# A decoder block on one core: the first pair's channel tiles share each piece of x, the rows come behind x, and turned values, tables and weight sums change places in the written order

## The chip, the cores and the metric

The kernel runs on one core of one Trainium2 chip. The metric is the device time of one execution in microseconds (us), the median over runs; lower is better.

## What is computed

One decoder block on a sequence of 1024 tokens with 1024 channels, in float32:

```python
h = rms_norm(x, mix_norm_g)
proj = h @ w_in                                   # 1024 -> 5888
z_a, q, k, v, gate_logits = split(proj)
y_a = chunked_spatial_gating(gelu(z_a), gmlp_norm_g, w_spatial, b_spatial)
q, k = apply_partial_rope(q, cos, sin), apply_partial_rope(k, cos, sin)
y_b = dilated_mixture_attention(q, k, v)          # 3 groups of 4 heads
merged = sigmoid(g_A) * (y_a @ w_branch_a) + sigmoid(g_B) * (y_b @ w_branch_b)
x = x + merged @ w_out
h2 = rms_norm(x, ffn_norm_g)
a, val = split(h2 @ w_up)                         # 1024 -> 2 x 2816
x = x + (gelu(causal_dwconv3(a)) * val) @ w_down
return rms_norm(x, final_norm_g)
```

In the spatial gating, `z_a` splits into `u` and `v`; `v` is RMS-normed over its 768 channels, mixed along 128 positions by a lower triangular matrix, and multiplied into `u`. The rotation (rope) turns the first 16 of 64 dimensions of q and k by tables of sines and cosines of the positions.

## The kernel before

**Operands in two parts.** TensorE multiplies in a float format shorter than float32, so each operand is split into a high part (ACT copies it into the short format) and a remainder (DVE, sometimes GpSimd, subtracts). Three matmuls per product, `PASSES`, take high x high, high x remainder and remainder x high. A weight tile or a tile of x must therefore pass through DMA, ACT and DVE before all three can run.

**Pairs and Strassen products.** The input projection is cut into 23 pairs of 128 columns. For most pairs a Winograd-Strassen scheme forms seven products P1 to P7 of quarter matrices, each of 12 matmuls of 128x512 (`in_product`, L512). Their left operands (A11, A12, A22, S1 to S4) are the normed x or sums of its quarters, their right ones are quarters of the pair's weights or sums of those (`weight_sums`, L270: three subtractions on DVE for P6, one for P4). `in_ahead` (L326) loads weights ahead and makes the operands of the next products; `in_split` (L300) gives the two halves of one such operand as two calls.

**The first two pairs are plain.** The left operands need the norm of x, which is not known at the start. So pairs 0 and 1 multiply raw x (times the gain), without Strassen, and the row scale is applied later, when the values are turned. Each pair has two channel tiles i = 0, 1 and two token halves h = 0, 1; `plain_step` (L575) issues the three matmuls of one piece of x, a [128 channels x 512 tokens] tile `x_half(kt, h)` of 256 KB. `raw_left` (L456) splits a piece. Beside this the rows of x (the other layout) are loaded into `rows_of`, ACT squares and sums them (`square_row`, L377), GpSimd takes the root (`root`, L384), DVE puts the scales on a diagonal (`diagonal`, L392), eight matmuls spread them over the partitions (`spread`, L401), and DVE scales x in place (`scale_x`, L468).

**An order written out by hand.** TensorE's order is that of the program everywhere. DVE's and ACT's are too from the start to product i = 10 (`ORDERED`), and again from the end of the mixing to `end_order(last_b)` (L2063); in between, and after, a scheduler chooses. `beginning` (L1069) writes the first part, then the loop from L1235 calls for each product i `in_ahead`, `in_product` and `meanwhile(i)` (L1186). Pair 2 (`FIRST`) has i = 0 to 6 (P1, P2, P6, P7, P5, P4, P3), pair 3 has i = 7 to 13 (P1, P6, P2, P7, P5, P4, P3). An engine works its list in order: an instruction that waits holds all behind it.

**Ticks.** `tick` (L213) is called twice in each product, after 6 and after 12 matmuls, and runs what `after(lag, fn)` has put there. So the turned values are placed: `turn_v` (L631) has TensorE transpose four 128x128 blocks into one of two PSUM banks (`tr_tile`), and ACT empties it into V (two instructions of L641 for pairs 0 and 1, one of L646 for pair 2). `norm_v` (L650), `spatial` (L655) and the rotation (`rope`, L729, with four stores on SP) are placed the same way.

**Tables.** `rot_tables` (L2236) makes a chain of 39 small steps on DVE (L2253), the last of which are two sines on ACT; 16 wide copies on ACT (L2299, `wide`); and four turns (`turns`: four transposes, L2316, and a copy by ACT, L2317). `some(n)` takes the next n steps of the chain.

**The up-projection.** It uses the same seven products per tile of 128 columns (`up_product`, L1838; `up_ahead` for loads and operands). `beginning_up` writes products 0 to 22 by hand. In a hand-written stretch remainders on DVE go to a list, `waiting`, and `low(n)` issues n of them; `end_order` issues the rest and ends the stretch. Products i = 23 to 29 are P6 of tile 4, P1 of 5, P7 and P5 of 4, P2 of 5, P4 and P3 of 4.

Of the kernel before, what the change touches and what calls it, by code (L numbers as in the profile page):

```python
# [20 lines left out]
P = 128  # L21
# [72 lines left out]
def block_kernel(  # L94
# [259 lines left out]
    raws[0, 0] = wt.tile([P, KT, P], F32, name="wr_0_0", tag="wr")  # L354
    for k in range(2):
        ks = slice(k * QK, (k + 1) * QK)
        nc.sync.dma_start(raws[0, 0][:, ks], w_in[0][:, ks])
        load_x(0, range(k * QK, (k + 1) * QK))
    in_load(0, 1)
    load_x(1, range(QK))  # L360
    load_rows(0)
    load_x(1, range(QK, KT))
# [212 lines left out]
    def plain_step(n, h, i, k, kt):  # L575
# [7 lines left out]
        for p, (w, a) in enumerate(PASSES):  # L583
            nc.tensor.matmul(
                acc, plain_ops[n, k, i][:, w, kt, :], raw_x[h, k * QK + kt][:, a, :],
                start=k == 0 and kt == 0 and p == 0,
                stop=k == 1 and kt == QK - 1 and p == 2,
                skip_group_check=True,
            )
# [131 lines left out]
    def turned(n):  # L721
# [24 lines left out]
        after(4, rope)  # L746
# [322 lines left out]
    def beginning():  # L1069
# [5 lines left out]
        chain = iter(chain)  # L1075

        def some(n):
            for _, fn in zip(range(n), chain):
                fn()
# [78 lines left out]
        product(1, 0, 1)  # L1158
# [23 lines left out]
        return some, wide, turns, a22  # L1182

    late = {}

    def meanwhile(i):  # L1186
# [6 lines left out]
        elif i == 2:  # L1193
            for _, lo in late["S1"]:
                lo()
            late["P4"] = in_split(FIRST, "P4")
            in_ready["op"] += 1
            late["P4"][0]()
        elif i == 3:
            late["P4"][1]()  # L1200
# [3 lines left out]
            for hi, _ in late["S4"]:  # L1204
                hi()
        elif i == 4:
            in_ahead(i, 9, 3)
            for _, lo in late["S4"]:
                lo()
            x_stack.close()  # L1210
# [4 lines left out]
            for b in range(0, NB, 2):  # L1215
                after(3 + b // 2, lambda b=b: turn_v(1, C[1], b))
                after(7 + b // 2, lambda b=b: turn_v(0, C[0], b))
        elif i in (5, 6):
            in_ahead(i, 9, 4)
        elif i == 7:  # L1220
            some(15)
        elif i == 9:
            some(99)
            for fn in wide:
                fn()
        elif i in (11, 12):
            turns.pop(0)()
# [6 lines left out]
    some, wide, turns, a22 = beginning()  # L1234
    for i, (n, name) in enumerate(in_order):  # L1235
        in_ahead(i, 9, 4 if i > ORDERED - 4 else 0)
# [1135 lines left out]
```

## Time and profile before

| what | value |
|---|---|
| median of 3 runs | 1392.97 us (1392.63 to 1394.66) |
| the profiled execution | 1394.24 us, span from its first to its last instruction 1392.5 us |
| mean granted TensorE clock | 0.995 |
| busy: TensorE, DVE, ACT, GpSimd | 1367.2, 1032.1, 653.9, 297.6 us |
| DMA | 237.01 MB, mean 170 GB/s |

PE is TensorE's matmuls, PEld its weight loads, DVE the vector engine, ACT the scalar engine, POOL GpSimd, SP the engine that issues most DMAs. A row of the order of time has the start in us, the length in us, engine, line, operation, output and inputs, shape, count of merged instructions, and in brackets the idle time of the engine before it with what ended it. In the chain of waits, "start, length, what". A matmul's length overlaps the next one's, so rates are read from start to start.

### The profile page before, as it was taken

How to read it: one execution, taken by the hardware profiler on the slowest of the kernel's cores; microseconds unless marked ns; L12 is line 12 of the kernel's file. 1: busy time of each engine (PE TensorE's matmuls, PEld its weight loads, DVE VectorE, ACT ScalarE, POOL GpSimd, SP SyncE). 2: the span in 40 equal slices, each digit the busy share in tenths (PEclk: the TensorE clock that was granted, in tenths of full speed). 3: DMA queues.
4: the chain of work that ended last, by engine and by line, in shares of the span. 5: the costliest groups of instructions: out<-in, count | busy, mean ns of one | idle time of the engine just before them, and what ended most of it. 6: DMA issues, size and time to landing. Idle time of an engine off the chain costs nothing.

```text
span 1392.5 us, 19210 instructions
## 1 busy us (share of the span) xinstructions
PE 1367.2 (98%) x6434; PEld 1131.8 (81%) x6434; DVE 1032.1 (74%) x1880; ACT 653.9 (47%) x1289; POOL 297.6 (21%) x295
## 2 busy tenths in 40 slices
PE   8979999999999999999999999999999999999997
PEld 7867788888888888888788887888888888888886
DVE  7967677686887987867889887766766667675674
ACT  7663255555554332634646443433333335455453
POOL 0111000000231000120001136555566553000002
PEclk9999999999999999999999999999999999999999
DMA  9423535354435987694843132333333327986563
GB/s 362 78 65 107 181 112 166 113 163 141 135 121 193 330 295 257 218 299 141 285 132 105 38 113 107 106 106 105 103 107 118 121 84 244 392 312 228 194 208 121
DMA packets 143875, 237.01 MB, mean 170 GB/s; under 512 B 13728, under 2 KB 57504, under 8 KB 143776
## 3 DMA queue, kind: packets, MB, share of 16 engines
q1 hardware_dynamic: 141248, 231.53, 49.5%
q0 software_dynamic: 1088, 2.10, 0.9%
q10 hardware_dynamic: 1440, 2.16, 0.4%
q8 instruction: 51, 0.84, 0.3%
q14 instruction: 48, 0.39, 0.1%
HBM read 167.77 MB, written 64.29 MB: 167 GB/s over the span
## 4 chain that ended last, share of the span: by engine, by line
PE 83%; DVE 6%; issue 3%; ACT 3%; DMA 2%; POOL 1%; SPq 0%; POOLq 0%; DVEq 0%; ACTq 0%
PE in_P L523 26%; PE uP L1849 18%; PE dn L2106 13%; PE up L1849 7%; PE pa L1322 5%; PE wo_P L1683 4%; PE pu L864 2%; PE pu L1829 2%; PE pb L1322 2%; DMA X<-in_xt_dram 1%; PE pp L848 1%; PE sc L809 1%; PE sc L810 1%; PE pm L673 1%; POOL fm_f L2227 1%
## 5 line engine op out<-in xcount | busy, mean ns | idle before, releaser
L523 PE MATMUL in_P<-R,G 128*128 128x512 f32 x1008 | 245.6, 396 | 0.0
L523 PEld LDWEIGHTS in_P<-R,G 128*128 128x128 f32 x1008 | 186.2, 189 | 36.3
L2106 PE MATMUL dn<-R 128*128 128x512 f32 x924 | 209.6, 389 | 0.0
L2106 PEld LDWEIGHTS dn<-R 128*128 128x128 f32 x924 | 173.5, 188 | 36.0
L168 ACT ACTIVATE R<-up 128x512 fp32r<-128x512 f32 x130 | 78.4, 627 | 118.6 <-DVE up L277 40.9
L307 ACT ACTIVATE G<-wr 128x512 fp32r<-128x512 f32 x126 | 79.0, 628 | 106.6 <-PE in_P L523 68.4
L523 PE MATMUL in_P<-G,G 128*128 128x512 f32 x504 | 123.8, 397 | 1.2 <-DVE C L550 1.2
L1849 PE MATMUL uP<-G,R 128*128 128x512 f32 x504 | 121.5, 390 | 1.8 <-DVE Y L1870 1.6
L1849 PE MATMUL up<-G,R 128*128 128x512 f32 x504 | 121.5, 391 | 0.1
L1849 PE MATMUL uP<-R 128*128 128x512 f32 x504 | 121.1, 389 | 0.0
L308 DVE TENSOR_TENSOR G<-wr,G 128x512 fp32r<-128x512 f32 x126 | 88.2, 700 | 33.5 <-ACT G L307 32.6
L1849 PEld LDWEIGHTS uP<-G,R 128*128 128x128 f32 x504 | 94.4, 188 | 22.5 <-DVE Y L1870 2.1
L1849 PEld LDWEIGHTS up<-G,R 128*128 128x128 f32 x504 | 94.6, 188 | 21.0 <-POOL R L169 0.6
L523 PEld LDWEIGHTS in_P<-G,G 128*128 128x128 f32 x504 | 94.1, 190 | 20.9 <-issue 1.8
L1849 PEld LDWEIGHTS uP<-R 128*128 128x128 f32 x504 | 94.6, 188 | 19.6
L169 POOL TENSOR_TENSOR R<-up,R 128x512 fp32r<-128x512 f32 x55 | 84.0, 1527 | 74.6 <-ACT R L168 74.6
L169 DVE TENSOR_TENSOR R<-up,R 128x512 fp32r<-128x512 f32 x75 | 62.3, 833 | 19.1 <-ACT R L168 18.9
L168 ACT ACTIVATE R<-db 128x512 fp32r<-128x512 f32 x77 | 48.1, 626 | 56.8 <-PE dn L2106 46.0
L169 DVE TENSOR_TENSOR R<-db,R 128x512 fp32r<-128x512 f32 x77 | 53.9, 703 | 26.0 <-ACT R L168 25.9
L1322 PE MATMUL pa<-R,G 128*128 128x512 f32 x288 | 67.9, 389 | 0.0
L523 PE MATMUL in_P<-G 128*128 128x512 f32 x252 | 62.4, 394 | 1.2 <-ACT G L307 1.2
L1322 PEld LDWEIGHTS pa<-R,G 128*128 128x128 f32 x288 | 54.1, 188 | 11.2
(279 smaller groups left out, 2398.2 us busy)
## 6 DMA issues: line engine op xcount, KB each, us to landing
wr<-in_w_in_dram SPq DMA_DIRECT2D x45, 512.0 KB, 4.3
up<-in_w_up_dram SPq DMA_DIRECT2D x44, 512.0 KB, 3.6
dA<-gd SPq DMA_DIRECT2D x55, 256.0 KB, 5.0
wd<-in_w_down_dram SPq DMA_DIRECT2D x44, 256.0 KB, 5.2
wT<-wd SPq DMA_DIRECT2D x44, 256.0 KB, 3.8
dS<-gS SPq DMA_DIRECT2D x44, 256.0 KB, 4.2
db<-wT SPq DMA_DIRECT2D x44, 256.0 KB, 4.5
gd<-Y SPq DMA_DIRECT2D x42, 256.0 KB, 2.0
```

The lines of the kernel that those rows point to most:

```text
L168: nc.scalar.activation(hi, src, AF.Copy)
L169: fn = lambda: lo_eng.tensor_tensor(lo, src, f32(hi), ALU.subtract)
L307: lambda: nc.scalar.activation(op[:, 0], src, AF.Copy),
L308: lambda: nc.vector.tensor_tensor(op[:, 1], src, f32(op[:, 0]), ALU.subtract),
L523: nc.tensor.matmul(acc, op[:, w, kt, :], left[LEFT[name], kt][:, a, :], start=opened and i == 0, stop=i == len(HIGH_FIRST) - 1, skip_group ...
L673: nc.tensor.matmul(pm[:, o : o + P], v[:, c * P : (c + 1) * P], wspT[:, c * 2 // 3, :], start=True, stop=True,)
L864: nc.tensor.matmul(pu[:, h * HD : (h + 1) * HD], self.pT[:, i, :], vt[:, h * HD : (h + 1) * HD], start=i % n == 0, stop=i % n == n - 1,)
L1322: nc.tensor.matmul(acc, unit[a][kt // 4][:, kt % 4, :], two(R, 8 * h + kt)[:, b, :], start=n == 0 and i == 0, stop=n == len(kts) - 1 and i ...
L1683: nc.tensor.matmul(acc, left[LEFT[name], kt][:, a, blk * P : (blk + 1) * P], out_ops[s][:, w, :], start=name not in SHARED and kt == 0 and ...
L1829: nc.tensor.matmul(acc, plain_up[which, k][:, w, kt, :], left[f"A{h + 1}{k + 1}", kt][:, a, :], start=n == 0 and i == 0, stop=n == KT - 1 ...
L1849: nc.tensor.matmul(acc, op[:, w, kt, :], left[LEFT[name], kt][:, a, :], start=opened and i == 0, stop=i == len(HIGH_FIRST) - 1, skip_group ...
L2106: nc.tensor.matmul(accs[blk], dops[s][:, 0, a, blk * P : (blk + 1) * P], dops[s][:, 1, w, :], start=SEQ[j] not in CONTINUES and kt == 0 an ...
```

## The change

- The weights of pair 0 arrive in pieces of two k-tiles (128 KB), alternating between its two channel tiles, each followed by one piece of the first half of x; the matmuls of both channel tiles on a piece are interleaved. All of the second half of x follows, and only then the rows of x.
- The steps of the tables are spread over the pieces (26 steps in the beginning instead of 23), the rest comes in `meanwhile(6)` instead of (7). The warm-up has 9 calls instead of 12. All four weights of pair 1 are split ahead of the second half's last product; the spread of the row scales comes 3 matmuls later in that product, and in pair 1's second tile rather than in its first.
- P3 of pair 2 is split in `meanwhile(3)` and (4), P1 of pair 3 in (4) and (5), P6 of pair 3 in (6).
- The turned values of pairs 0 and 1 start a tick later and are bunched differently; norms and mixing come one tick later, the rotation 10 ticks after its product instead of 4.
- The 16 wide copies are divided over i = 10 and 11, the four turns of the tables over i = 12 to 15.
- In the up-projection the hand-written order ends behind product 29 instead of 22.

```diff
-    raws[0, 0] = wt.tile([P, KT, P], F32, name="wr_0_0", tag="wr")
-    for k in range(2):
-        ks = slice(k * QK, (k + 1) * QK)
-        nc.sync.dma_start(raws[0, 0][:, ks], w_in[0][:, ks])
-        load_x(0, range(k * QK, (k + 1) * QK))
-    in_load(0, 1)
-    load_x(1, range(QK))
+    for i in range(2):
+        raws[0, i] = wt.tile([P, KT, P], F32, name=f"wr_0_{i}", tag="wr")
+    for kt in range(0, KT, 2):
+        ks = slice(kt, kt + 2)
+        for i in range(2):
+            nc.sync.dma_start(raws[0, i][:, ks], w_in[i][:, ks])
+            load_x(0, (kt + i,))
+    load_x(1, range(KT))
     load_rows(0)
-    load_x(1, range(QK, KT))
     in_load(1, 0)
     in_load(1, 1)
...
-                    after(9 + 2 * b, lambda b=b: norm_v(b))
-                    after(14 + 2 * b, lambda b=b: spatial(b))
+                    after(10 + 2 * b, lambda b=b: norm_v(b))
+                    after(15 + 2 * b, lambda b=b: spatial(b))
...
-        after(4, rope)
+        after(10, rope)
...
-        warm_up(12)
-        some(9)
-        for k in range(2):
-            weight(0, k, 0)
-            for kt in range(k * QK, (k + 1) * QK):
+        warm_up(9)
+        for i in range(2):
+            for k in range(2):
+                plain_op(0, k, i)
+        for kt in range(KT):
+            k, n = divmod(kt, QK)
+            if kt % 2 == 0:
+                for i in range(2):
+                    op, ks = plain_ops[0, k, i], slice(n, n + 2)
+                    src = raws[0, i][:, kt : kt + 2]
+                    nc.scalar.activation(op[:, 0, ks], src, AF.Copy)
+                    if i == 0:
+                        raw[0, kt][0]()
+                    nc.vector.tensor_tensor(op[:, 1, ks], src, f32(op[:, 0, ks]), ALU.subtract)
+                    if i == 0:
+                        raw[0, kt][1]()
+            else:
                 raw_parts(0, kt)
-            product(0, 0, 0, (k,))
-        some(2)
-        weight(0, 0, 1)
-        weight(0, 1, 1)
-        product(0, 0, 1)
-        for kt in range(QK):
+                some(2)
+            for p in range(3):
+                for i in range(2):
+                    plain_pass(0, 0, i, k, n, p)
+        for kt in range(KT):
             raw_parts(1, kt)
-        square_row(0, 0)
-        square_row(0, 1)
-        raw_parts(1, 4)
-        raw_parts(1, 5)
-        square_row(0, 2)
-        raw_parts(1, 6)
-        raw_parts(1, 7)
-        square_row(0, 3)
+            some(1)
+        plain_final(0, 0, 0)
+        plain_final(0, 0, 1)
+        for b in range(4):
+            square_row(0, b)
         load_rows(1)
         root(0)
-        plain_final(0, 0, 0)
-        plain_final(0, 0, 1)
         product(0, 1, 0)
-        some(12)
+        some(10)
         diagonal(0)
         weight(1, 0, 0)
         weight(1, 1, 0)
+        weight(1, 0, 1)
+        weight(1, 1, 1)
         product(0, 1, 1, (0,))
+        plain_step(0, 1, 1, 1, 0)
         bc0 = spread(0)
-        product(0, 1, 1, (1,))
+        for kt in range(1, QK):
+            plain_step(0, 1, 1, 1, kt)
...
-        weight(1, 0, 1)
-        weight(1, 1, 1)
-        for n in range(KT):
-            plain_step(1, 0, 0, n // QK, n % QK)
-            if n == 5:
-                bc1 = spread(1)
+        product(1, 0, 0)
+        plain_step(1, 0, 1, 0, 0)
+        bc1 = spread(1)
...
     def meanwhile(i):
...
         elif i == 3:
...
+            split_of(FIRST, "P3")
+            late[FIRST, "P3"][0]()
         elif i == 4:
-            in_ahead(i, 9, 3)
+            late[FIRST, "P3"][1]()
             for _, lo in late["S4"]:
                 lo()
+            in_ahead(i, 9, 0)
+            split_of(FIRST + 1, "P1")
+            late[FIRST + 1, "P1"][0]()
...
             for b in range(0, NB, 2):
-                after(3 + b // 2, lambda b=b: turn_v(1, C[1], b))
-                after(7 + b // 2, lambda b=b: turn_v(0, C[0], b))
-        elif i in (5, 6):
+                after(min(4 + b // 2, 6), lambda b=b: turn_v(1, C[1], b))
+                after(8 + b // 2, lambda b=b: turn_v(0, C[0], b))
+        elif i == 5:
+            in_ahead(i, 9, 0)
+            late[FIRST + 1, "P1"][1]()
+        elif i == 6:
+            in_ahead(i, 9, 3)
+            some(steps_left() - 1)
+        elif i == 7:
             in_ahead(i, 9, 4)
-        elif i == 7:
-            some(15)
         elif i == 9:
             some(99)
-            for fn in wide:
+        elif i == 10:
+            for fn in wide[:8]:
                 fn()
-        elif i in (11, 12):
-            turns.pop(0)()
+        elif i == 11:
+            for fn in wide[8:]:
+                fn()
+        elif i in (12, 13, 14, 15):
             turns.pop(0)()
...
-        in_ahead(i, 9, 4 if i > ORDERED - 4 else 0)
+        in_ahead(i, 9, 4 if i > ORDERED - 4 and i != 7 else 0)
...
     beginning_up()
-    end_order(last_b)
...
             up_product(ff, name)
+            low(len(waiting))
+            if i == 29:
+                end_order(last_b)
```

`plain_pass` is the body of `plain_step` for one of its three matmuls; `split_of` calls `in_split` and counts it; `steps_left` is the number of steps of the tables still to come.

More of the change, by code (lines that the diff above doesn't have):

```diff
@@ L573, in plain_op, with plain_pass @@
         )
-    def plain_step(n, h, i, k, kt):
+    def plain_pass(n, h, i, k, kt, p):
         if (n, h, i) not in plain_banks:
@@ L582, in plain_step @@
         acc = plain_banks[n, h, i]
[L583 to L589, printed above, removed]
+        w, a = PASSES[p]
+        nc.tensor.matmul(
+            acc, plain_ops[n, k, i][:, w, kt, :], raw_x[h, k * QK + kt][:, a, :],
+            start=k == 0 and kt == 0 and p == 0,
+            stop=k == 1 and kt == QK - 1 and p == 2,
+            skip_group_check=True,
+        )
+    def plain_step(n, h, i, k, kt):
+        for p in range(3):
+            plain_pass(n, h, i, k, kt, p)
     def plain_final(n, h, i):
@@ L1074, in beginning @@
         )
-        chain = iter(chain)
         def some(n):
-            for _, fn in zip(range(n), chain):
-                fn()
+            for _ in range(min(n, len(chain))):
+                chain.pop(0)()
         def weight(n, k, i):
@@ L1100, in splits @@
                     fn()
-        warm_up(12)
-        some(9)
-        for k in range(2):
-            weight(0, k, 0)
-            for kt in range(k * QK, (k + 1) * QK):
-                raw_parts(0, kt)
-            product(0, 0, 0, (k,))
-        some(2)
-        weight(0, 0, 1)
-        weight(0, 1, 1)
-        product(0, 0, 1)
-        for kt in range(QK):
-            raw_parts(1, kt)
-        square_row(0, 0)
-        square_row(0, 1)
-        raw_parts(1, 4)
-        raw_parts(1, 5)
-        square_row(0, 2)
-        raw_parts(1, 6)
-        raw_parts(1, 7)
-        square_row(0, 3)
+        warm_up(9)
[15 more added lines that the diff above has]
+            else:
+                raw_parts(0, kt)
+                some(2)
+            for p in range(3):
+                for i in range(2):
+                    plain_pass(0, 0, i, k, n, p)
+        for kt in range(KT):
+            raw_parts(1, kt)
+            some(1)
[3 more added lines that the diff above has]
+            square_row(0, b)
         load_rows(1)
         root(0)
-        plain_final(0, 0, 0)
-        plain_final(0, 0, 1)
         product(0, 1, 0)
-        some(12)
+        some(10)
         diagonal(0)
@@ L1157, in beginning @@
                 x_sum_dma(3, kt // 2)
-        product(1, 0, 1)
+        for n in range(1, KT):
+            plain_step(1, 0, 1, n // QK, n % QK)
         plain_final(1, 0, 0)
@@ L1181, in beginning, with split_of @@
             x_sum_dma(4, k)
-        return some, wide, turns, a22
+        return some, lambda: len(chain), wide, turns, a22
     late = {}
+    def split_of(n, name):
+        late[n, name] = in_split(n, name)
+        in_ready["op"] += 1
     def meanwhile(i):
@@ L1195, in meanwhile @@
                 lo()
-            late["P4"] = in_split(FIRST, "P4")
-            in_ready["op"] += 1
-            late["P4"][0]()
+            split_of(FIRST, "P4")
+            late[FIRST, "P4"][0]()
         elif i == 3:
-            late["P4"][1]()
+            late[FIRST, "P4"][1]()
             for _, lo in a22:
@@ L1233, in block_kernel @@
     )
-    some, wide, turns, a22 = beginning()
+    some, steps_left, wide, turns, a22 = beginning()
     for i, (n, name) in enumerate(in_order):
-        in_ahead(i, 9, 4 if i > ORDERED - 4 else 0)
+        in_ahead(i, 9, 4 if i > ORDERED - 4 and i != 7 else 0)
         if PAIRS[n][0] == "zu" and name == "P1":
```

## The prediction

> **What bounds the kernel now.** I read the busy table of the page first, then all the waits of TensorE, then the busy time by stretch, and last the order of time around each wait.
>
> ```profile
> PE 1367.2 (98%) x6434; PEld 1131.8 (81%) x6434; DVE 1032.1 (74%) x1880; ACT 653.9 (47%) x1289; POOL 297.6 (21%) x295
> ```
>
> TensorE is busy for 98% of the span, so only 25 us could go without taking matmuls out, and the change takes none out. The waits of TensorE over the whole run say where those are (us in all, times, longest):
>
> ```profile
> core 0 of [0], span 1392.5 us
> engine line waited for: us in total, times, longest us
> PE vt L636 <- ACT V L641: 5.1, 1, 5.1
> PE rot L2316 <- ACT YC L2317: 3.4, 2, 2.7
> PE pl L584 <- DVE R L463: 2.0, 4, 1.2
> PE warm L373 <- POOL ident masks.py:199: 1.7, 1, 1.7
> PE uP L1849 <- DVE Y L1870: 1.6, 1, 1.6
> PE in_P L523 <- DVE C L550: 1.2, 3, 0.6
> PE in_P L523 <- ACT G L307: 1.2, 1, 1.2
> PE uP L1849 <- DVE Y L1881: 0.5, 1, 0.5
> ```
>
> Six of these eight rows stand where the change rewrites the order: the turned values (vt), the tables (rot), the first products (pl), the last operand of pair 2 (in_P on ACT) and the two of the up-projection (uP). They come to 13.8 us. What lies behind them is read by stretch (busy time and count of PE, PEld, DVE, ACT, POOL; granted clock; DMA share; GB/s):
>
> ```profile
> 10.00:30.00 20.00, 19.10 (x84) 14.19 (x83) 14.17 (x34) 16.74 (x29) 1.23 (x2) 1.00 1.03 403
> 30.00:70.00 40.00, 40.00 (x183) 33.22 (x182) 38.59 (x63) 28.27 (x54) 6.30 (x6) 1.00 0.48 116
> 80.00:90.00 10.00, 7.75 (x34) 6.69 (x35) 6.71 (x18) 6.21 (x14) 1.60 (x4) 0.66 0.19 55
> ```
>
> From 10 to 30 us the DMA is full (403 GB/s). From 30 to 70 DVE is, with 38.59 of 40, so an earlier TensorE is worth there only what DVE is earlier too. From 80 to 90 the granted clock is down to 0.66: a long wait of TensorE also costs clock afterwards. What matmuls cost when nothing holds them is read from a product of 12:
>
> ```profile
> 100.11 2.89 PE L523 MATMUL in_P<-G,G 128*128 128x512 f32 x12
> 102.84 0.60 PE L2316 MATMUL rot<-ident,YC 128*128 128x128 f32 x4
> ```
>
> From start to start that is 2.73 us, 0.2275 each.
>
> **The change part by part.**
>
> *A. The first pair shares the pieces of x.* Order of time on TensorE, and one row of the chain that ended last:
>
> ```profile
> 6.05 0.47 PE L584 MATMUL pl<-R,G 128*128 128x512 f32 x1
> 7.74 3.04 PE L584 MATMUL pl<-R,G 128*128 128x512 f32 x12 [1.21 <-DVE R L463]
> 10.99 8.33 PE L584 MATMUL pl<-R,G 128*128 128x512 f32 x35 [0.21 <-DVE R L463]
> 19.16 2.88 PE L584 MATMUL pl<-G 128*128 128x512 f32 x12
> ...
> 26.25 2.91 PE L584 MATMUL pl<-G 128*128 128x512 f32 x12
> 29.00 1.14 PE L405 MATMUL rs_bc<-C,ones 128*128 128x128 f32 x8
> ```
>
> ```profile
> 13.23 7.81 DMA X<-in_xt_dram
> ```
>
> ```profile
> 10.19 2.74 DVE L463 SCALAR_TENSOR_TENSOR R<-X,chan,R 128x512 fp32r<-128x512 f32 x4
> 12.83 0.29 DVE L2253 TENSOR_TENSOR ones<-ones 128x128 f32<-128x128 f32 x1
> ```
>
> The 48 matmuls of the first token half run from 6.05 to 19.16, 13.1 us. At 0.2275 each they need 10.9: 2.2 us are lost. The next 24 take 7.09 us (19.16 to 26.25) and need 5.46: 1.6 lost, because their fifth piece of x lands at 13.23 + 7.81 = 21.04.
>
> In the new order the same 4.25 MB of weights and x are sent up to that piece, but not the 2 MB of rows. At 403 GB/s 2 MB are 5.2 us: it lands at 15.8, the eighth at 17.8, the rows at 23.0 and pair 1's weights (1 MB) at 25.6, well before their first matmul. Going back from 15.8, the last piece of the first half lands near 12.5, and TensorE, which now spends six matmuls (1.36 us) on a piece, needs it at 15.6. So DMA stops being the bound, and DVE is next. For two pieces it has two remainders of x at 0.685, two remainders of weights at half the old width, and two steps of the tables, at most 0.29 each and here taken as 0.25. A half-width remainder is not in the trace; the row of 128x128 (0.29) and that of 128x512 (0.685) bound it, and I take 0.4, since 256 is nearer to the first. That is 1.37 + 0.8 + 0.5 = 2.7 us against 2.72 of TensorE: even. At 0.685 it would be 3.2, and half the gain would go. I take the first half as ending at 17.0 instead of 19.16.
>
> In the second half one channel tile alone follows, 0.68 us a piece, and DVE needs 0.685 + 0.25 = 0.93: DVE sets the pace, eight pieces from 15.8 end at 23.2, and the 24 matmuls at 23.7 (before 26.25). Then ten table steps (2.5) and the four diagonals stand on DVE until about 27, while the squares of the later rows (the last lands at 23.0; ACT, POOL) are done near 26.3: the spread of the row scales comes at 27.3 against 29.00, with 15 matmuls ahead of it instead of 12 (0.7). That is 2.4 earlier for TensorE. DVE, which binds the next 40 us, has done two more weight remainders by then but three more table steps. I put down **-1.9**, between -3.8 (all that is lost) and +1 (half-width pieces at full price on DVE and on ACT). The nine warm-up matmuls instead of twelve end before the first operand is there, as they did; nothing is put down.
>
> *B. The last operand of pair 2 (P3) is split a product earlier.* Its high part stood on ACT behind a gelu that waits for DVE: the 1.2 us of the row above. Now it is ahead of it, and the remainder is first on DVE. What is late next is DVE's remainders of S4, which also start 1.2 earlier. **-1.2** (0 to -1.3).
>
> *C. Turned values and weight sums.* TensorE, then ACT:
>
> ```profile
> 76.57 0.60 PE L636 MATMUL vt<-ident,C 128*128 128x128 f32 x4
> 82.25 1.11 PE L636 MATMUL vt<-ident,C 128*128 128x128 f32 x4 [5.08 <-ACT V L641]
> 83.02 2.91 PE L523 MATMUL in_P<-R,G 128*128 128x512 f32 x6
> 85.72 1.75 PE L636 MATMUL vt<-ident,C 128*128 128x128 f32 x8
> 87.22 1.65 PE L523 MATMUL in_P<-R,G 128*128 128x512 f32 x6
> ```
>
> ```profile
> 80.84 0.63 ACT L307 ACTIVATE G<-wr 128x512 fp32r<-128x512 f32 x1 [2.89 <-DVE wr L277]
> 81.38 1.55 ACT L641 ACTIVATE V<-vt,rs_x 128x256 f32<-128x256 f32 x4
> ```
>
> Three turns in the same product need a third bank of two; it is freed by ACT's copy (L641), which stands behind the high part of pair 3's P6, which waits for three sums on DVE. The wait is 5.1. After it six matmuls take 2.70 (83.02 to 85.72) where six at 0.227 need 1.36: 1.3 more. In the new order product 6 has two turns for two banks, and nothing waits on ACT ahead of their copies. The same wait of ACT for the sums comes back in product 7, ahead of the copies of its two middle turns: from the end of product 6 DVE has an add and three sums (4 x 0.7), ACT then the high part (0.63) and a copy (0.78), 4.2 in all, while TensorE has 12 matmuls and two turns, 3.7. So the first of the three turns at the end of that product waits 0.5, and the third, for its bank, about as long: 1.0. The table steps that went from meanwhile(7) to meanwhile(6) are behind the sums on DVE and hold nobody there. **-5.4** of 6.4 (-6.4 to -2).
>
> [...]
>
> *D. The tables in four turns of their own products, the wide copies in two.*
>
> ```profile
> 106.17 0.66 PE L2316 MATMUL rot<-ident,YC 128*128 128x128 f32 x4 [2.73 <-ACT YC L2317]
> 107.01 4.61 PE L523 MATMUL in_P<-G,G 128*128 128x512 f32 x12 [0.19 <-DVE C L550]
> ```
>
> ```profile
> 101.84 3.28 ACT L2299 ACTIVATE YC<-ones 128x128 f32<-128x128 f32 x16
> ```
>
> The second turn of a pair waits for ACT's copy of the first, which stands behind 16 wide copies (3.28). Both such waits are 3.4. The product behind the longer one takes 4.61 where the one of 100.11 takes 2.89: 1.7 more. With a whole product (2.73) between two turns, the copy of one is done before the next; eight wide copies (1.64) fit in one. **-4.9** of 5.1 (-5.1 to -2.5). ACT remains the fullest engine here, and I leave 0.2.
>
> *E. The hand order of the up-projection goes on to i = 29.* Until now the order of DVE was free from i = 23, and it took work of later products ahead of adds that free a bank:
>
> ```profile
> 845.10 1.77 DVE L1808 TENSOR_TENSOR own<-Y 128x512 f32<-128x512 f32 x1 [2.17 <-POOL Y L1882]
> ```
>
> DVE waits 2.17 us for GpSimd in front of the add (L1870) for which TensorE then waits 1.6; with L1881's 0.5 it is 2.1. In the new order the add is written ahead of that sum, and each remainder behind its product's add. **-2.0** (-2.1 to +1: waits of the same kind in the fixed order).
>
> *F. What is moved and costs nothing.* The rotation goes from 4 to 10 ticks after its product, three products later, and with it four stores on SP:
>
> ```profile
> 130.86 0.59 SPq L744 DMA_DIRECT2D kd<-C  x1
> ...
> 155.40 1.24 SPq L784 DMA_DIRECT2D q<-qd  x2
> ```
>
> The last of them is out at 131.45 and is read from 155.40. Three products are 8.2 us, and 16.4 if each carries as much again of turns and mixing; 131.45 + 16.4 = 147.9 leaves 7.5 us for the landing. The norms and mixing of the gated branch move by one tick together, so their distance stays.
>
> **Sum:** -1.9 - 1.2 - 5.4 - 4.9 - 2.0 = -15.4. The profiled execution took 1394.24 us (span 1392.5), 1.27 above the median of 1392.97; the gain counts from the median: 1377.6. If every lost microsecond named went (3.8 + 1.2 + 6.4 + 5.1 + 2.1 = 18.6), it would be 1374.4. Behind 150 us the waits are so small that TensorE passes the gain on to the end.
>
> **The rivals.**
>
> *R1, the stall only moves.* ACT's wait of 2.89 for the sums holds the bank in product 7 in full, because DVE is later there than I think. Then 2.9 stay and the half clock with them (1.3), as after the 2.73 of part D: 4.2 in place of the 1.0 that the sum already leaves, so 1380.8. [...] For it speaks the same order on ACT (sums, high part, copies), against it that two banks are free at the start of the product.
>
> *R2, the small pieces feed slower.* Each weight load is cut into four of 128 KB. If the first 3 MB moved at half of 403 GB/s, they would take 7.8 us longer, the last piece would land at 20.3 and the first half end at 21.7, 2.5 behind the old order; part A is then +2.5 to +4, I take +3: 1382.5. The row at 403 GB/s, made of pieces of 256 and 512 KB, speaks against it. [...]
>
> *R3, the fixed order of E waits for GpSimd itself,* once for 2.17 with nothing able to pass: +1 instead of -2, 1380.6.
>
> *R4, slower.* From 110 us to 660 us the order of DVE and ACT is free, and moved rotations change what it is made from. There are 24 attention blocks. If TensorE waited 0.8 us in each, it would be +19.2: 1396.8. It decides from 15.4 / 24 = 0.64 a block. The longest wait on DVE in that stretch is 0.6, once in three (the row of L550), and nothing in those blocks is rewritten: little speaks for it.
>
> *R5, it does nothing:* the moved steps are late all the same, 1393.
>
> *R6, the slow product of part D has another cause than the wait ahead of it,* so its 1.7 stays: 1379.3. [...]
>
> **How the numbers follow.** Forecast 0.55, R1 0.13, R2 0.09, R3 0.08, R4 0.08, R5 0.04, R6 0.03. The range goes from below the ceiling of 1374.4 (a little more where the spreads and turns close up as well) to beyond R2: 1373.5 to 1384. That leaves out R4 and R5. Within 0.2% (2.8 us, about what a measurement of this kernel can tell from no change) is R5's 0.04, slower R4's 0.08, faster the rest, 0.88.
>
> **What would show it.** In the waits of TensorE: vt on L641 and rot on L2317 under 1.5 us together and the granted clock at 1.00 from 80 to 120 us (C, D); the first spread of row scales near 27.3 and the fifth piece of the second half landing near 15.8 (A); no ACT wait of P3 (B); none of L1870 or L1881 over 0.3 (E). A wait on L641 of 2 to 3 us in the product after pair 2's last says R1; a first half of x that lands after 15 says R2; many waits of 0.5 and more between 150 and 660 say R4.

## The result: 1382.66 us, and the profile after

| | before | changed |
|---|---|---|
| median | 1393.07 us (1392.63 to 1394.66, 4 runs) | 1382.66 us (1381.99 to 1386.08, 4 runs) |
| ratio to before, 95% interval | 1 | 0.9928 (0.991 to 0.9946) |
| profiled execution, span | 1394.24, 1392.5 us | 1382.45, 1380.7 us |

The change makes the kernel faster, by 10.4 us between the medians and by 11.8 between the two profiled spans. The forecast was 1377.6 with a range of 1373.5 to 1384.0: the direction is right, the time is inside the range, and 5 us of the gain are missing. In the changed kernel the later lines have other numbers: L636 and L641 (turned values) are L640 and L645, L2316 (turns of the tables) is L2344, L1849 (products of the up-projection) is L1875, L1870 and L1881 (the adds) are L1896 and L1907, L1862 (the copy of P4) is L1888, L1780 (the second gelu's line) is L1806.

The busy table of the page of the changed kernel, and below it the waits of its TensorE on which the rest rests (us in all, times, longest):

```profile
PE 1364.7 (99%) x6428; PEld 1129.2 (82%) x6428; DVE 1033.8 (75%) x1884; ACT 655.8 (47%) x1294; POOL 300.8 (22%) x295
```

```profile
PE uP L1875 <- POOL R L169: 2.1, 1, 2.1
...
PE rs_bc L405 <- DVE C L397: 1.0, 1, 1.0
PE uP L1875 <- ACT R L168: 0.6, 1, 0.6
PE vt L640 <- ACT V L645: 0.5, 1, 0.5
...
PE vt L640 <- ACT C L539: 0.3, 1, 0.3
```

The six rows of before that came to 13.8 us are gone but for 0.8 of vt. Two long rows are new: the first spread waits 1.0 for the diagonals, and a product of the up-projection (uP) waits 2.1 for a remainder on GpSimd. The busy time by stretch, in the columns that the prediction gave:

```profile
10.00:30.00 20.00, 18.99 (x88) 15.39 (x87) 17.56 (x49) 17.43 (x30) 1.23 (x2) 1.00 1.03 394
30.00:70.00 40.00, 39.59 (x177) 32.04 (x176) 37.95 (x61) 29.11 (x56) 6.30 (x6) 1.00 0.51 129
80.00:90.00 10.00, 9.51 (x54) 7.80 (x53) 7.53 (x18) 9.42 (x22) 3.95 (x7) 1.00 0.21 53
```

The DMA still runs at 394 GB/s at the start, DVE is still full from 30 to 70 us (37.95 of 40), and from 80 to 90 us the granted clock is 1.00 where it was 0.66.

**A ledger by marks.** TensorE's order is that of the program, so the same product can be found in two traces, and the difference of its starts says how much has been won up to there. Three marks of before that were not shown yet (P3 of pair 2, P6 of pair 3, and the end of P3 of pair 3, where the next row begins), then the order of time of the changed kernel at the start and at the same marks:

```profile
73.09 1.66 PE L523 MATMUL in_P<-G 128*128 128x512 f32 x6 [1.16 <-ACT G L307]
...
89.50 1.63 PE L523 MATMUL in_P<-R,G 128*128 128x512 f32 x6
...
116.01 0.38 PE L673 MATMUL pm<-wspT,V 128*128 128x128 f32 x2
```

```profile
5.51 11.87 PE L584 MATMUL pl<-R,G 128*128 128x512 f32 x48
17.22 2.88 PE L584 MATMUL pl<-G 128*128 128x512 f32 x12
...
27.32 1.16 PE L405 MATMUL rs_bc<-C,ones 128*128 128x128 f32 x8 [1.01 <-DVE C L397]
...
71.07 3.42 PE L523 MATMUL in_P<-G 128*128 128x512 f32 x12 [0.19 <-DVE C L552]
...
80.92 0.66 PE L640 MATMUL vt<-ident,C 128*128 128x128 f32 x4 [0.49 <-ACT V L645]
81.34 1.64 PE L523 MATMUL in_P<-R,G 128*128 128x512 f32 x6
...
100.63 0.60 PE L2344 MATMUL rot<-ident,YC 128*128 128x128 f32 x4
```

At P3 of pair 2 the changed kernel is 73.09 - 71.07 = 2.0 ahead, at P6 of pair 3 89.50 - 81.34 = 8.2, and at the end of pair 3's P3 116.01 - 100.63 = 15.4. By then before has done three turns more (0.36 each, as from 97.42 to the next product at 97.78), so 14.3 are really won. At the up-projection it is still ahead by that much and a little more: the product that begins a period of seven there starts at 827.46 before and at 812.45 after, 15.0. Two periods later:

```profile
827.46 3.03 PE L1849 MATMUL uP<-G,R 128*128 128x512 f32 x12 [0.20 <-ACT R L168]
...
869.10 2.88 PE L1849 MATMUL uP<-G,R 128*128 128x512 f32 x12
```

```profile
812.45 3.02 PE L1875 MATMUL uP<-G,R 128*128 128x512 f32 x12
...
844.76 1.20 PE L1875 MATMUL uP<-R 128*128 128x512 f32 x4 [0.59 <-ACT R L168]
848.07 2.65 PE L1875 MATMUL uP<-R 128*128 128x512 f32 x8 [2.10 <-POOL R L169]
850.52 3.99 PE L1875 MATMUL uP<-opx,R 128*128 128x512 f32 x12
...
857.09 2.88 PE L1875 MATMUL uP<-G,R 128*128 128x512 f32 x12
```

Before needs 869.10 - 827.46 = 41.64 for the fourteen products, the changed kernel 857.09 - 812.45 = 44.64. Part E, which was to give 2.0, gives back 3.0. That is most of what the forecast missed, and the experiments begin there.

### The profile page after: what moved, and what is told of

Read it like the earlier page. It is cut to its first block, busy times and chain, and to the rows that moved or that the text cites. A ratio compares the mean times of both kernels' runs of the same rounds, so it can differ in the third digit from the quotient of the medians.

```text
span 1380.7 us, 19226 instructions
## 1 busy us (share of the span) xinstructions
PE 1364.7 (99%) x6428; PEld 1129.2 (82%) x6428; DVE 1033.8 (75%) x1884; ACT 655.8 (47%) x1294; POOL 300.8 (22%) x295
## 4 chain that ended last, share of the span: by engine, by line
PE 80%; DVE 8%; DMA 5%; issue 3%; ACT 2%; POOL 1%; SPq 1%; POOLq 0%; DVEq 0%; ACTq 0%
PE in_P L523 23%; PE uP L1875 17%; PE dn L2134 13%; PE up L1875 7%; PE pa L1348 5%; PE wo_P L1709 4%; PE pu L868 2%; PE pu L1855 2%; PE pb L1348 2%; DMA wd<-in_w_down_dram 1%; DMA YC<-in_x_dram 1%; PE pp L852 1%; DMA wT<-wd 1%; DMA X<-in_xt_dram 1%; DVE wd L1019 1%
## 5 line engine op out<-in xcount | busy, mean ns | idle before, releaser
L1875 PE MATMUL uP<-R 128*128 128x512 f32 x504 | 122.0, 391 | 2.7 <-POOL R L169 2.1
L1875 PE MATMUL up<-G,R 128*128 128x512 f32 x504 | 121.5, 391 | 0.5 <-ACT R L168 0.3
L1875 PE MATMUL uP<-G,R 128*128 128x512 f32 x504 | 121.6, 390 | 0.0
L1875 PEld LDWEIGHTS uP<-R 128*128 128x128 f32 x504 | 94.7, 188 | 23.1 <-POOL R L169 2.5
L1875 PEld LDWEIGHTS up<-G,R 128*128 128x128 f32 x504 | 94.5, 188 | 21.8 <-ACT R L168 0.8
L1875 PEld LDWEIGHTS uP<-G,R 128*128 128x128 f32 x504 | 94.5, 188 | 20.5 <-ACT R L168 0.4
L1348 PEld LDWEIGHTS pa<-R,G 128*128 128x128 f32 x288 | 54.1, 188 | 11.2
```

The costliest lines, as they stand in the source:

```text
L1348: nc.tensor.matmul(acc, unit[a][kt // 4][:, kt % 4, :], two(R, 8 * h + kt)[:, b, :], start=n == 0 and i == 0, stop=n == len(kts) - 1 and i ...
L1875: nc.tensor.matmul(acc, op[:, w, kt, :], left[LEFT[name], kt][:, a, :], start=opened and i == 0, stop=i == len(HIGH_FIRST) - 1, skip_group ...
```

## The experiments

All times are medians, and all ratios are to the kernel before on the same chip, with 95% intervals. The theories of part E, in the numbering of the expectations: theory 1, the place where the hand order ends costs (scheduler and written order meet there); theory 2, as it was first put, the loss belongs to tile 5, whose remainders go to GpSimd, and stays at products 30 to 33 wherever the order ends; theory 2a, which came later, the written order itself costs: ACT's high part of P7 of tile 5 (product 32) now stands behind the second gelu of tile 4. The rows of the changed kernel on which theory 2a rests:

```profile
843.56 0.63 ACT L1806 ACTIVATE Y<-Y 128x512 f32<-128x512 f32 x1 [2.24 <-DVE Y L1817]
844.10 0.61 ACT L168 ACTIVATE R<-t 128x512 fp32r<-128x512 f32 x1
844.27 1.29 POOL L1904 TENSOR_TENSOR Y<-Y 128x512 f32<-128x512 f32 x1 [2.27 <-ACT Y L1806]
...
845.52 1.27 POOL L1908 TENSOR_TENSOR Y<-Y 128x512 f32<-128x512 f32 x1
846.75 1.27 POOL L169 TENSOR_TENSOR R<-t,R 128x512 fp32r<-128x512 f32 x1
```

and the same step in the free order of before:

```profile
846.36 0.63 ACT L168 ACTIVATE R<-t 128x512 fp32r<-128x512 f32 x1 [3.41 <-POOL t L275]
847.06 1.57 POOL L169 TENSOR_TENSOR R<-t,R 128x512 fp32r<-128x512 f32 x1 [0.74 <-ACT R L168]
...
858.51 0.63 ACT L1780 ACTIVATE Y<-Y 128x512 f32<-128x512 f32 x1 [1.80 <-DVE Y L1791]
```

In before the high part (R from t) and its remainder are done by 848.63, ten us ahead of that gelu, and the product that reads them is the eleventh behind the one at 827.46 (it starts at 860.85). In the changed kernel ACT waits 2.24 for DVE's taps, does the gelu, and only then the high part. The gelu also releases two products on GpSimd (1.29 and 1.27), which stand ahead of the remainder there. The remainder is done at 848.02, and TensorE's third pass of P7 starts at 848.07.

**Part E alone, on the kernel before.**

```diff
     beginning_up()
-    end_order(last_b)
...
             up_product(ff, name)
+            low(len(waiting))
+            if i == 29:
+                end_order(last_b)
```

> The kernel before with only the last part of the change: the hand-written order of the up-projection ends behind product 29. Theory 1: plus 2.9 us, about 1396. My prediction had minus 2.0 for this part alone: 1391.

Measured: 1396.25 (11 runs) against 1393.62 (17), ratio 1.0022 (1.0013 to 1.0031): 2 to 4 us slower. Its waits of TensorE have the rows of the changed kernel to the tenth:

```profile
PE uP L1849 <- POOL R L169: 2.1, 1, 2.1
...
PE uP L1849 <- ACT R L168: 0.6, 1, 0.6
```

So E costs by itself, whatever the start did. In its profiled run the cost is 1.5 us (span 1394.0 against 1392.5), in the changed kernel's 3.0. By the marks it is the same: E alone takes 43.09 us for the fourteen products (827.47 to 870.56), 1.5 more than before's 41.64. The difference is clock. Busy time by stretch behind the same wait of 2.10, first the changed kernel, then E alone:

```profile
848.00:854.00 6.00, 5.93 (x19) 4.75 (x20) 3.52 (x4) 1.05 (x2) 4.64 (x5) 0.72 0.17 66
```

```profile
863.00:869.00 6.00, 5.92 (x26) 4.85 (x27) 3.51 (x4) 1.00 (x2) 4.63 (x5) 1.00 0.17 67
```

In 6 us there were 19 matmuls at a granted clock of 0.72 in the one and 26 at 1.00 in the other.

**The changed kernel without E.** The end of the hand order goes back ahead of the loop.

```diff
     beginning_up()
+    end_order(last_b)
...
-            low(len(waiting))
-            if i == 29:
-                end_order(last_b)
```

> The changed kernel with the hand-written order of the up-projection ended ahead of product 23 again, as before the change. In the changed kernel TensorE loses 5.9 us at products 30 to 33, right behind the new end; before the change it lost 3.1 at products 23 to 28, right behind the old one. Theory 1 (the end costs: the free order that follows takes later work ahead of what TensorE waits for): the loss goes back to about 3 at products 23 to 28, and the time is 2.9 below the changed kernel, about 1379.8 us. Theory 2 (the loss at 30 to 33 belongs to tile 5, whose remainders go to GpSimd, wherever the order ends): it stays, and the time is about 1382.7.

Measured: 1381.54 (1378.99 to 1383.29, 5 runs), ratio 0.991 (0.9896 to 0.9925). The old waits are back (1.7 and 0.5 for the adds), the new one is gone, and the fourteen products take 41.68 us, as in before. So theory 2 in its first form falls, for the loss did not stay with tile 5; theories 1 and 2a both allow this run. The median is only 1.1 below the changed kernel, and the intervals overlap, so by the times alone this run does not settle it. Its profiled run (span 1381.1) has 3.0 us of waits of in_P for DVE's L550, with an order up to there that is the same as the changed kernel's, which waited 0.2 in that row. Such waits differ by 2.8 us between these two runs; the rows of the stretch, and E alone, say what E does.

**The end of the hand order moved on,** to product 36, and to the last product of the up-projection's loop.

```diff
-            if i == 29:
+            if i == 36:
```

> The changed kernel with the hand-written order ended seven products later, behind 36. Theory 1: products 30 to 36 run without waits, and a loss of 0 to 6 us stands behind 36; DVE has less to do from tile 5 on, so rather 1 to 3: 1378 to 1380. Theory 2: the 5.9 us stay at 30 to 33 and the time at about 1382.7.

```diff
-            if i == 29:
+            if i == last_p2:
```

> The changed kernel with the hand-written order kept up to the last product whose order was free, so that it does not end in the middle of the up-projection. Theory 1: the 5.9 us go and nothing takes their place: 1376.8. Theory 2, or a rival in which a fixed order makes ACT's copies wait behind gelus in every tile: as the changed kernel or slower, 1383 to 1400.

Measured: 1382.7, ratio 0.9929 (0.9914 to 0.9943), and 1387.4, ratio 0.9955 (0.9943 to 0.9967). The order of time on TensorE, of the first and then of the second:

```profile
846.03 3.41 PE L1875 MATMUL uP<-R 128*128 128x512 f32 x8 [3.00 <-POOL R L169]
...
868.79 2.11 PE L1875 MATMUL uP<-R 128*128 128x512 f32 x8 [1.77 <-POOL R L169]
```

```profile
848.06 2.09 PE L1875 MATMUL uP<-R 128*128 128x512 f32 x8 [2.99 <-POOL R L169]
849.99 2.93 PE L1875 MATMUL uP<-opx,R 128*128 128x512 f32 x12
```

With the end seven products later the wait stays at P7 of tile 5 and comes once more at P7 of tile 6. With no end in the loop it stays as well. Theory 1, which expected 1378 to 1380 and 1376.8 here, falls. The free order that follows a hand-written one is not what costs: replacing more of it gains nothing, and replacing all of it in the loop costs 4 to 5 us more.

**The operands asked for one product earlier.** If the place of the high part is the cause, it must help to write it earlier: in products 23 to 29 operands are made five products ahead instead of four.

```diff
-            up_ahead(i + 9, i + 4)
+            up_ahead(i + 9, i + (5 if i < 30 else 4))
```

> The changed kernel, with each operand of products 23 to 29's look-ahead made one product earlier (five ahead instead of four). Theory 2a (in the fixed order ACT's copy for P7 of tile 5 stands behind the second gelu of tile 4, so GpSimd takes its two products with 1.3 us each first, and the remainder of P7 comes 2 to 3 us late): the copy is now ahead of that gelu, the wait of 2.1 on GpSimd's remainder and most of the 5.9 us at products 30 to 33 go: 1377 to 1379. Theory 1 (the end of the fixed order costs in itself): the loss stays, 1382.7.

Measured: 1381.25, ratio 0.9913 (0.99 to 0.9927). The time is not told apart from the changed kernel's (the intervals overlap), and theory 2a had expected 1377 to 1379. In the trace the wait at P7 is gone, and another has come, at a product for which the earlier operand is too early. Order of time, ACT and then TensorE:

```profile
831.96 0.63 ACT L168 ACTIVATE R<-up 128x512 fp32r<-128x512 f32 x1 [4.31 <-DVE up L280]
832.49 0.58 ACT L1888 ACTIVATE t<-up 128x512 f32<-128x512 f32 x1
...
833.12 4.61 PE L1875 MATMUL up<-G,R 128*128 128x512 f32 x12 [2.30 <-ACT t L1888]
```

ACT waits 4.31 us for a sum on DVE, and the copy behind it (L1888) holds the bank that the next product needs. This is the mechanism of theory 2a at another place: an instruction that waits in a queue holds what stands behind it.

**Five ahead in products 28 and 29 alone,** where the high part of P7 is due and the early sum is not.

```diff
-            up_ahead(i + 9, i + 4)
+            up_ahead(i + 9, i + (5 if i in (28, 29) else 4))
```

> The changed kernel with operands made five ahead only at products 28 and 29. Theory 2a: P7 of tile 5 then has its copy ahead of tile 4's second gelu, so the 2.1 on GpSimd's remainder goes, and P4's operand isn't made so early that its sum holds the copy that frees a bank (the 2.3 us that came in its place when all of products 23 to 29 looked five ahead): 5 of the 5.9 us at products 30 to 33 go, 1377.5. Rival: another wait of 2 to 3 us takes their place again, 1380.

Measured: 1379.59 (1379.11 to 1381.26, 4 runs), ratio 0.9901 (0.9887 to 0.9914), span 1377.6. It has the lowest median of all, 3.1 under the changed kernel's, though the intervals still overlap a little; theory 2a had expected 1377.5, its rival, another wait in the same place, 1380. The wait for GpSimd is gone, but one of before's has come back in its place, for the add of a bank:

```profile
853.86 3.02 PE L1875 MATMUL uP<-G,R 128*128 128x512 f32 x12 [2.17 <-DVE Y L1896]
```

The fourteen products take 41.71 us (812.15 to 853.86), 2.9 less than in the changed kernel and no less than in before's 41.64. So all of E's loss is removed and none of its hoped-for gain is had.

**The other parts, one by one on the kernel before.** The start alone (A: loads, shared pieces, order of `beginning`):

```diff
...
+    for kt in range(0, KT, 2):
+        ks = slice(kt, kt + 2)
+        for i in range(2):
+            nc.sync.dma_start(raws[0, i][:, ks], w_in[i][:, ks])
+            load_x(0, (kt + i,))
+    load_x(1, range(KT))
     load_rows(0)
...
-            some(15)
+            some(steps_left() - 1)
```

> The kernel before with only the new beginning: the order of loads, the interleaved first pair, the table steps among them and pair 1's weights ahead. In the changed kernel TensorE is 2.0 us earlier at pair 2's P3 than before. If that is all passed on: 1391.3. If DVE, full from 30 to 70 us, or the wait on turned values at 82 us swallows it: 1393.3.

Measured: 1392.03 (11 runs), ratio 0.9993 (0.9984 to 1.0002): 1 us, and not told apart from nothing by the times. In its trace P3 of pair 2 starts at 71.94 where before has 73.09, 1.15 earlier.

**The turned values alone** (B and C: splits, turns and weight sums; the table steps stay in product 7, the tables as before):

```diff
...
             for b in range(0, NB, 2):
-                after(3 + b // 2, lambda b=b: turn_v(1, C[1], b))
-                after(7 + b // 2, lambda b=b: turn_v(0, C[0], b))
+                after(min(4 + b // 2, 6), lambda b=b: turn_v(1, C[1], b))
+                after(8 + b // 2, lambda b=b: turn_v(0, C[0], b))
...
         elif i == 7:
+            in_ahead(i, 9, 4)
             some(15)
```

> The kernel before with only the splits of P3, P1 and P6 and the turned values at their new places (tables as before). The two traces put its share at 6.3 us at the start of pair 3's P6; my prediction had 1.2 + 5.4 = 6.6. Both: about 1386.9. If the wait only moves to product 7 with the half clock behind it: 1390.

Measured: 1394.63 (11 runs), ratio 1.0007 (0.9999 to 1.0016). The largest term of the prediction, done alone, brings nothing. The order of time on DVE, ACT and TensorE shows why:

```profile
84.05 0.69 DVE L308 TENSOR_TENSOR G<-wr,G 128x512 fp32r<-128x512 f32 x1 [4.10 <-ACT G L307]
...
93.11 0.69 DVE L280 TENSOR_TENSOR wr<-wr 128x512 f32<-128x512 f32 x1
...
93.83 0.63 ACT L307 ACTIVATE G<-wr 128x512 fp32r<-128x512 f32 x1 [5.11 <-DVE wr L280]
...
95.24 1.11 PE L636 MATMUL vt<-ident,C 128*128 128x128 f32 x4 [4.14 <-ACT V L641]
```

DVE stands idle for 4.10 us in the product before, then does the table steps among the sums of the next operand, whose last is done only at 93.80. ACT waits 5.11 for it, with the copy that frees the bank behind it, and TensorE waits 4.14. The wait that the change took out at 82 us is back at 95, and the tables' own waits (rot) have grown from 3.4 to 5.6.

**The same with the table steps one product earlier,** in DVE's idle time:

```diff
         elif i == 6:
             in_ahead(i, 9, 3)
+            some(15)
         elif i == 7:
             in_ahead(i, 9, 4)
-            some(15)
```

> The run with only the splits and the turned values moved, and beside that the 15 table steps put from behind product 7 to behind product 6, as the change has them. Theory 3 (left behind product 7, the steps stand on DVE ahead of the sum for pair 3's P4, ACT's high part of P4 waits 5.1 us for it, and behind that the copies that free the banks of the turned values: the wait of 5.3 at 82 us came back as 4.1 at 95): now they fill the time in which DVE waits for ACT, the wait at 95 us goes, 1394.6 - 4.3 - 1.4 for the half clock = 1389. The tables' own waits (5.6 there) stay. Rival (16 wide copies on ACT hold the banks, not DVE's steps): the wait stays, 1394.6.

Measured: 1388.86, ratio 0.9966 (0.9953 to 0.9978): one moved line is worth 5 to 6 us (1.0007 against 0.9966). The wait of vt is 0.5; the two of rot stay (5.7).

**The tables alone** (D):

```diff
-        after(4, rope)
+        after(10, rope)
...
-            for fn in wide:
+        elif i == 10:
+            for fn in wide[:8]:
+                fn()
+        elif i == 11:
+            for fn in wide[8:]:
                 fn()
-        elif i in (11, 12):
-            turns.pop(0)()
+        elif i in (12, 13, 14, 15):
             turns.pop(0)()
```

> The kernel before with only the tables' wide copies divided over products 10 and 11, their four turns over 12 to 15, and the rotation six ticks later. The two traces put its share at 6.1 us; my prediction had 4.9. 1387.2 to 1388.4. If the half rate behind the wait has another cause than the wait, 1.7 stay: 1389.

Measured: 1388.82, ratio 0.9966 (0.9954 to 0.9978). That is 3 to 6 us. No wait of rot is left, and the products behind the turns at 107.44 and 112.66 us take 3.01 and 3.03 where before had 4.61.

**B, C and D together, without A and E.** The three diffs above in one kernel.

> The last kernel with the tables' copies and turns divided as well: the change without its new beginning and without the longer hand order. If the parts in the middle give 12.4 us together, as the two traces have it: 1381 to 1382, and the beginning is worth the 1 to 2 us that lie between this and the changed kernel less 2.6. If they only add up as they did alone (plus 1.4 and minus 4.4): 1390.

Measured: 1381.77 (1380.98 to 1384.57), ratio 0.9921 (0.9907 to 0.9934), 9 to 13 us. Its marks, in the order of time on TensorE:

```profile
71.90 3.42 PE L523 MATMUL in_P<-G 128*128 128x512 f32 x12
...
82.16 1.64 PE L523 MATMUL in_P<-R,G 128*128 128x512 f32 x6
...
101.47 0.60 PE L2331 MATMUL rot<-ident,YC 128*128 128x128 f32 x4
```

Against before's marks they give each part a price: B 73.09 - 71.90 = 1.2; C 89.50 - 82.16 less that, 6.1; D 116.01 - 101.47 - 1.1 for the three turns, less 7.3, 6.1. The changed kernel's own marks lie 0.8 earlier throughout (71.07, 81.34, 100.63): that is A. Each mark is of one profiled run, and the clock differs between runs, as the last section shows: by the times D alone is worth 4.4 to 4.7, less than its 6.1 here.

## Why the prediction was right in direction and 5 us off

| part | forecast | by the marks | |
|---|---|---|---|
| A, the start | -1.9 | -0.8 (alone -1.15) | mis-sized, by another path |
| B, P3 split earlier | -1.2 | -1.2 | as worked out |
| C, turned values | -5.4 | -6.1 | mechanism right |
| D, tables | -4.9 | -6.1 | mechanism right, clock in part luck |
| E, hand order to 29 | -2.0 | +3.0 | wrong sign |
| sum | -15.4 | -11.2 | spans -11.8, medians -10.4 |

The time is inside the range because what E and A lack (5.0 and 1.1) is partly made up by C and D, which gave 1.9 more than forecast.

*A.* The first half ends at 17.22 where 17.0 was worked out. DVE sets the pace there, as the prediction said (busy for 9.90 of the 10 us from 10 to 20), and a half-width remainder takes 0.42 where 0.4 was taken. The pieces land later than worked out: the fifth piece of the second half at 17.23 instead of 15.8, the last row that the first spread needs at 24.36 instead of 23.0. The spread comes at 27.32 where 27.3 was forecast, but that is luck, for the path to it is another one. The prediction had DVE as the later of two, with table steps and diagonals until about 27, and the rows' squares done near 26.3. Two rows of the chain that ended last, then DVE in the changed kernel, then DVE in before:

```profile
16.57 7.79 DMA YC<-in_x_dram
...
25.56 7.38 DMA YC<-in_x_dram
```

```profile
26.98 0.87 DVE L397 TENSOR_SCALAR C<-ident,rs_x 128x128 f32<-128x128 f32 x4 [2.06 <-POOL rs_x L388]
...
37.38 1.29 DVE L420 SCALAR_TENSOR_TENSOR R<-X,R 128x512 fp32r<-128x512 f32 x2 [0.64 <-ACT R L419]
```

```profile
28.65 0.87 DVE L397 TENSOR_SCALAR C<-ident,rs_x 128x128 f32<-128x128 f32 x4
```

DVE is done with its table steps at 24.92 (the second half's remainders ended at 22.09, not at 23.2) and waits 2.06 us for the root on GpSimd, which waits for the squares of the row that lands at 24.36. In before DVE had no wait there: its own steps held the diagonals. So the rows, which the change puts behind all of x, now hold the first spread, and the prediction had them as the earlier of the two. TensorE is 1.7 earlier at the spread, with three matmuls more behind it (2.4 in all), but only 0.8 is left at P3. DVE, which is nearly full behind it (37.95 of the 40 us from 30 to 70), starts the diagonals 1.67 earlier (26.98 against 28.65) and loses 0.64 of that again at 37.38: the second four rows have landed at 32.94 (before 31.44), and ACT's work behind their scales is late. In A alone the same two figures are 1.61 and 0.38, which leaves 1.2, and the mark says 1.15. The prediction had warned that an earlier TensorE is worth only what DVE is earlier, and yet carried 1.9 of the 2.4.

*B and C.* B is exact. In C the remaining waits are 0.5 and 0.3 where 1.0 was left (the 0.3 at the end of product 6, where none was forecast; the 3.7 for 12 matmuls and two turns in that working has 0.5 a turn, and a turn takes 0.36), and the half clock of 80 to 90 us (0.50 granted from 83.0 to 85.7 us in before, 1.00 now) went with the wait, so nearly all of the 6.4 came. One step of the reasoning was right, but its weight was not seen: "The table steps that went from meanwhile(7) to meanwhile(6) are behind the sums on DVE and hold nobody there." They hold nobody there, but they would have held everything where they were. The turned values alone, with the steps left in place, are no gain at all (1.0007); with the steps moved the ratio is 0.9966. The prediction priced the parts one by one as if they could be added, and this pair can't.

*D.* The 0.2 that was left for ACT was not needed. The rest is how the loss was read: the prediction took the idle column for it (2.73), but from the first turn's start to the second's (102.84 to 106.17) 3.33 passed where a turn takes 0.36, so 3.0 were lost, another 0.5 before the product at 107.01, and 0.9 at the second such wait (111.46 to 112.75) instead of 0.69. That the 1.7 of half clock was there to be won is in part luck: in other runs the same wait is not followed by it (see R6).

*E.* Here the prediction failed. It read the wait right (an add that frees a bank, behind a sum that waits for GpSimd), and both its rows are gone, as "none of L1870 or L1881 over 0.3" asked. But it took the free order of before for a fault only, and looked at the one instruction that came out badly. The free order had also done the high part of tile 5's P7 and its remainder ten us ahead of the gelu; the written order puts the high part behind the gelu, and the remainder behind two products on GpSimd. R3 had the engine and the sign (GpSimd, +1), but with another instruction waiting and with the clock left out: it forecast 1380.6.

*The other rivals.* R1 is not seen: the wait in product 7 is 0.5, not 2.9. But the turned values alone show that it was one line away. R2 is refuted: the last piece of the first half lands at 12.99, not after 15. The DMA is only a little slower while the small pieces move: from 4 to 10 us it makes 312 GB/s, and 336 in before. R4 is not seen: the waits in the attention blocks are 0.3 at most. R6 did not come: with the wait gone in the tables alone, the slow product is gone. But the wait alone does not make a product slow either. In the turned values alone a wait of 2.75 at the same turn is followed by 12 matmuls in 3.00, in the order of time on TensorE:

```profile
105.98 0.66 PE L2328 MATMUL rot<-ident,YC 128*128 128x128 f32 x4 [2.75 <-ACT YC L2329]
106.39 3.00 PE L523 MATMUL in_P<-G,G 128*128 128x512 f32 x12
```

What else decides is not shown: half clock followed waits of 2.10, 2.30 and 2.73 here.

## What to carry to other kernels

A wait cleared in a written order can come back at the next place where a filler stands ahead of a needed instruction in a queue worked in order (here 5.08 us at 82 us came back as 4.14 at 95), so move the fillers into the idle time with it, and price such parts together. A forecast mark that is met does not show that the forecast path led to it, so look at what released it. Before a free stretch is replaced by a written one, list what the free order did early as well as what it did late. A wait named in the forecast that vanishes does not show the gain: measure the whole stretch from one mark to another in both traces.

## What was not expected of the hardware

Half clock does not follow from the length of a wait alone. The wait of 2.10 at P7 was followed by 0.72 in one kernel and by 1.00 in another (the rows stand above), at a price of 1.5 us. A wait of 2.99 (the hand order to the end) was followed by full rate, 12 matmuls in 2.93 and 1.00 granted from 848 to 853 us, and one of 2.30 (five ahead) by half, 12 in 4.61 and 0.66 granted from 833 to 838. The wait of 2.73 ahead of part D's product was followed by 4.61 in before, one of 2.75 there by 3.00 in the turned values alone. What beside the length decides, no run here shows.

Kernels that differ only behind 800 us differed before it as well: waits for DVE's L550 came to 0.2 us in one profiled run and 3.0 in another, with the same order. That is about as large as parts A and E, and why those two were settled by marks in the traces rather than by medians of a few runs.
